# Gathering diagonal blocks by DMA in a DeltaNet encoder block, with DVE's order and the inversion's place changed

## The chip, the cores and the metric

The kernel runs on one core of one Trainium2 chip. The core's engines are TensorE (PE, with its weight loads PEld), VectorE (DVE), ScalarE (ACT), GpSimd (POOL) and SyncE (SP); transfers are issued here from SP's queue and, for some, from ACT's. The metric is the device time of one execution in microseconds. The kernel before took a median of 1217.43 us in three runs (1215.95 to 1219.03).

## The reference

The input is one sequence of 1024 tokens with 1024 channels in float32. One layer is computed:

```
xn   = rmsnorm(x)
proj = xn @ w_in                     # 1024 x 2832: attention q, k, v; gated DeltaNet q, k, v, z; gates a, b
attn = windowed attention, 8 heads of 64, 2 key/value heads, window 128, bias and sink
gdn  = two gated DeltaNets (forward and backward), 4 heads of 128, chunks; rmsnorm, times silu(z)
h    = x + concat(attn, gdn) @ w_out
out  = rmsnorm(h + relu(rmsnorm(h) @ w_ffn_in)^2 @ w_ffn_out)
```

The part that the change touches is the preparation of the DeltaNet, for each chunk, head and direction:

```
decay = exp(gc[i] - gc[j])           # on and below the diagonal
A     = beta * (k k^T) * decay       # strictly below the diagonal
T     = inverse(I + A)
P     = (q k^T) * decay
```

T and P are then used by a scan over the chunks.

## The kernel before

The kernel works with chunks of 128 tokens, eight of them, four heads and two directions. Products are made in three float32r passes: each operand is split into a rounded part and a remainder, and `mm3` (lines 136 to 138) multiplies high by high, high by low and low by high. Banks of PSUM come in two groups of four, psA and psB.

After the norms, the gates and the projections of DeltaNet's k and q, `phases` runs two streams of Python generators woven together (`weave`). Each yields a cost after each piece; the stream whose sum of costs, divided by its weight, is smaller is traced next.

- The first stream (weight 145) traces 28 projections, each of 24 matmuls into a psA bank, each yielding 5.2: eight for DeltaNet's v (`proj_conv`; copied from PSUM by ACT at line 404, convolved by DVE at 383 and 385, Silu on ACT at 387, transposed at 424, scaled at 464), eight for z (`proj_z`; Silu from PSUM at 473), four for attention's keys and values and eight for its queries (`proj_attn`; PSUM is left by DVE at 491 for keys and values, at 509 for queries). `proj_attn` first zeroes the unused halves of two key tiles, on DVE (486).
- The second stream (weight 100) traces `prep`, `eliminate`, `diag_blocks` and `invert` for its steps 0 and 1 (chunks 0 to 3); steps 2 and 3 come later, beside attention. Its yields sum to 24 for `prep`, 25.9 for `eliminate` and 4.8 for `diag_blocks`.

`prep` goes over the chunks. For each it computes k k^T (649) and q k^T (651) in two psB banks, and for each direction the decay's exponents in another (656, 657); ACT takes the exponential (661), DVE makes A (665, tile `at`), stores it to a DRAM tensor `atd` (672), and multiplies the decay with q k^T (673, which also reads the second bank for the last time in direction 1), stored to `pd` (674). The four 32 x 32 blocks on A's diagonal are copied by ACT (670, four copies for each chunk and direction, each 32 partitions x 4 heads x 32) to a tile `diag` for each direction.

`eliminate` transposes `diag` in 32 x 32 blocks on DVE (682), so that all 32 blocks of a partition group lie along the free axis, and inverts them together in 31 steps of a product and a subtraction on DVE (691, 693). `diag_blocks` transposes the result back, in two forms (702, 703). `invert` combines the blocks to the full inverses with small products: it loads A from `atd` (724), multiplies 32 x 32 blocks (750), copies them out by ACT (753), writes the diagonal blocks in place by ACT and DVE (734), multiplies again (766, 770), and goes on to 64 x 64 blocks (792, 800).

The instructions are not issued as traced. At the end of tracing, a planner that simulates the time of each instruction puts every engine's instructions in an order: of those that are ready in the simulation, the one traced first. On the chip each engine, and each queue of transfers, follows its order without exception, and waits where the order has an instruction whose inputs are late. `tc.issue_after(i)` ties instructions behind `i` on the same engine in that order; `behind` does this for a list.

Of the kernel before, what the change touches and what calls it, by code (L numbers as in the profile page):

```python
# [14 lines left out]
ALU = mybir.AluOpType  # L15
AX = mybir.AxisListType

P = 128
# [55 lines left out]
def chain(*gens):  # L74
    for g in gens:
        yield from g


class Block:
# [187 lines left out]
    def gemm(self, ws, xs, pstag):  # L267
        ps = self.ps(pstag)
        for k in range(NK):
            self.mm3(ps, ws[0][:, k, :], ws[1][:, k, :], xs[k][:, 0], xs[k][:, 1], k == 0, k == NK - 1)  # L270
        return ps
# [205 lines left out]
    def proj_attn(self):  # L477
# [6 lines left out]
        self.kh, self.kl = [self.pg(dt=F32R) for _ in range(2)], [self.pg(dt=F32R) for _ in range(2)]  # L484
        for v, o in enumerate((up, lo)):
            nc.vector.tensor_copy(out=self.kl[v][o, :], in_=self.zero[o, :].to_broadcast([64, SEQ]))
        self.va = self.pg((P, NT, P))
# [154 lines left out]
    def prep(self):  # L642
        nc = self.nc
        self.diag = [self.pg((P, 32, 32)) for _ in range(2)]
        for c in range(NT):
            sl = slice(c * P, (c + 1) * P)
            gg, kq = self.ps("psB", (P, GH, P)), self.ps("psB", (P, GH, P))
# [4 lines left out]
            for d in range(2):  # L652
# [10 lines left out]
                for h in range(GH):  # L663
# [3 lines left out]
                                                   op0=ALU.mult, op1=ALU.mult)  # L667
                for q in range(4):
                    r = slice(32 * q, 32 * q + 32)
                    nc.scalar.copy(out=self.diag[d][r, :, 4 * c:4 * c + 4].rearrange("p i h -> p h i"),  # L670
                                   in_=at[r, :, r])
                nc.sync.dma_start(out=self.atd[c, :, d], in_=at)
                nc.vector.tensor_tensor(out=dec, in0=dec, in1=kq, op=ALU.mult)
                nc.sync.dma_start(out=self.pd[c, :, d], in_=dec)
                yield 1.5

    def eliminate(self):

        nc = self.nc
        m, t = self.dbl((P, 2, 32, 32)), self.dbl((P, 2, 32, 32))  # L680
        for d in range(2):
            nc.vector.transpose(out=m[:, d].rearrange("p a b -> p b a") if d else m[:, d], in_=self.diag[d])
        nc.gpsimd.memset(t.rearrange("p d a b -> p (d a b)"), 0.0)
# [23 lines left out]
    def invert(self, tt, steps):  # L707
# [10 lines left out]
        for i in steps:  # L718
# [3 lines left out]
            for d in range(2):  # L722
                a = both[:, d]
                nc.sync.dma_start(out=a, in_=self.atd[2 * i:2 * i + 2, :, d].rearrange("c p h x -> p c h x"))
                at.append(flat(a))
                mk = {(0, 1): self.wh, (0, 2): self.wl}.get((d, i))
                tt[d][i] = mk((P, 2, GH, P), F32) if mk else self.pg((P, 2, GH, P))
                nc.gpsimd.memset(tt[d][i].rearrange("p c h x -> p (c h x)"), 0.0)
# [17 lines left out]
            for n in range(8):  # L746
                for j in range(2):
                    for d in range(2):
                        s, e = pairs[d][j]
                        nc.tensor.matmul(px[blk(e), n, :], at[d][blk(s), n, blk(e)], ct[d][blk(s), :, 8 * i + n],  # L750
                                         start=True, stop=True)
            x32 = self.pt((P, 8, 32))
# [553 lines left out]
    def build(self):  # L1306
        tc, nc = self.tc, self.nc
        with (
# [14 lines left out]
            self.kvd = d("kvd", (NT, P, 2, GH, P))[:]  # L1323
            self.pd, self.atd = d("pd", (NT, P, 2, GH, P))[:], d("atd", (NT, P, 2, GH, P))[:]
            self.phases()

    def phases(self):
# [11 lines left out]
        for half in range(2):  # L1339
# [5 lines left out]
            else:  # L1345
# [16 lines left out]
        run(weave((chain(self.proj_conv(C_GV, "v"), self.proj_z(), self.proj_attn()), 145.0),  # L1362
                  (chain(self.prep(), self.eliminate(), self.diag_blocks(), self.invert(tt, (0, 1))), 100.0)))
        self.bias_table()
# [91 lines left out]
```

## Time and profile before

| what | us |
|---|---|
| median of 3 runs | 1217.43 (1215.95 to 1219.03) |
| profiled execution, whole | 1216.62 |
| its span, first to last instruction | 1214.9 |
| PE busy | 1171.8 |
| DVE busy | 855.4 |
| ACT busy | 610.2 |
| POOL busy | 560.5 |
| mean granted clock of TensorE | 0.989 of full |

In the profile a time of an instruction is counted from the first instruction of the execution. An engine's idle time before an instruction is put down to what ended it: "[1.73 <-DVE pt L673]" says that the engine was idle for 1.73 us until an instruction of DVE at line 673, which writes a tile `pt`, was done. Names are the program's own, without buffer numbers: psA and psB are the two groups of PSUM banks, pg, pt, sc, wr, wh, wl and dbl groups of buffers. An engine's name with a q stands for its sequencer, where transfers are issued. The granted clock is a share of TensorE's full clock.

### The profile page before, as it was taken

What the parts mean: (1) busy time and instruction counts of PE and PEld (TensorE: products, weight loads), DVE (VectorE), ACT (ScalarE), POOL (GpSimd) and SP (SyncE); (2) the same over time, 40 slices, a digit from 0 to 9 for tenths busy, and PEclk for the clock granted to TensorE, in tenths of its full rate; (3) what the DMA queues carried; (4) which work ended last, traced back from release to release, by engine and by line L of the source; (5) the groups of instructions that cost most, each with busy time, mean ns of one, the idle gap of its engine ahead of it and who ended that gap; (6) DMA issues with size and microseconds to landing.
All of it is one profiled execution on the core that took longest, in us unless ns stands there. A gap on an engine that the chain in (4) does not pass through costs nothing. (4 is left out here: it accounts for less than half of the span.)

```text
span 1214.9 us, 18460 instructions
## 1 busy us (share of the span) xinstructions
PE 1171.8 (96%) x6482; PEld 960.9 (79%) x6482; DVE 855.4 (70%) x1482; ACT 610.2 (50%) x1331; POOL 560.5 (46%) x470
## 2 busy tenths in 40 slices
PE   6999999899979989999999999999999999999997
PEld 5788878677868778888788888888878888888885
DVE  4676667994399986687855445454598796987976
ACT  6455588424385752134745454454555444334443
POOL 5354311223421224143854453635456565555695
PEclk9999999899989999999999999999999999999999
DMA  6134344433645567323143444344779535443323
GB/s 246 53 102 145 89 167 163 157 123 97 219 138 176 187 203 274 121 96 122 53 166 130 157 154 156 134 153 147 244 277 333 184 104 173 135 156 109 104 87 139
DMA packets 121630, 187.62 MB, mean 154 GB/s; under 512 B 11043, under 2 KB 64416, under 8 KB 121537
## 3 DMA queue, kind: packets, MB, share of 16 engines
q1 hardware_dynamic: 103876, 155.20, 38.7%
q10 hardware_dynamic: 17661, 31.24, 6.8%
q8 instruction: 51, 0.84, 0.3%
q14 instruction: 42, 0.34, 0.1%
HBM read 122.39 MB, written 63.49 MB: 153 GB/s over the span
## 5 line engine op out<-in xcount | busy, mean ns | idle before, releaser
L136 PE MATMUL psA<-pg,wh 128*128 128x512 f32 x416 | 165.6, 399 | 3.4 <-DVE pt L491 1.7
L138 PE MATMUL psA<-pg,wl 128*128 128x512 f32 x416 | 164.8, 396 | 0.0
L137 PE MATMUL psA<-pg,wh 128*128 128x512 f32 x416 | 164.5, 395 | 0.0
L124 POOL TENSOR_TENSOR wl<-wr,wh 128x512 fp32r<-128x512 f32 x44 | 67.0, 1544 | 156.1 <-ACT wh L123 126.9
L1225 DVE TENSOR_TENSOR pg<-pg 128x512 fp32r<-128x512 f32 x112 | 122.3, 1125 | 14.9 <-ACT pg L1224 14.9
L124 POOL TENSOR_TENSOR wh<-wr,wh 128x512 fp32r<-128x512 f32 x32 | 47.4, 1498 | 139.6 <-ACT wh L123 131.3
L1142 ACT ACTIVATE pt<-pt 128x512 f32<-128x512 f32 x64 | 40.4, 632 | 121.2 <-DVE pt L1132 121.1
L136 PE MATMUL psA<-pg,pg 128*128 128x512 f32 x256 | 98.7, 391 | 0.8 <-DVE pg L1270 0.8
L137 PE MATMUL psA<-pg,pg 128*128 128x512 f32 x256 | 99.3, 391 | 0.0
L138 PE MATMUL psA<-pg,pg 128*128 128x512 f32 x256 | 99.2, 389 | 0.0
L136 PEld LDWEIGHTS psA<-pg,wh 128*128 128x128 f32 x416 | 78.9, 190 | 20.9 <-ACT pt L473 2.1
L137 PEld LDWEIGHTS psA<-pg,wh 128*128 128x128 f32 x416 | 79.0, 190 | 18.0 <-issue 0.9
L138 PEld LDWEIGHTS psA<-pg,wl 128*128 128x128 f32 x416 | 78.9, 190 | 17.0
L124 POOL TENSOR_TENSOR pg<-wr,pg 128x512 fp32r<-128x512 f32 x48 | 73.8, 1571 | 38.1 <-ACT pg L123 38.1
L1224 ACT CAST pg<-pg 128x512 fp32r<-128x512 f32 x112 | 66.9, 620 | 38.0 <-DMA pg<-sd 31.3
L137 PE MATMUL psB<-pg,pg 128*128 128x512 f32 x192 | 74.9, 390 | 0.8 <-POOL pg L124 0.7
L138 PE MATMUL psB<-pg,pg 128*128 128x512 f32 x192 | 74.7, 389 | 0.0
L136 PE MATMUL psB<-pg,pg 128*128 128x512 f32 x192 | 74.7, 389 | 0.0
L1132 DVE TENSOR_TENSOR pt<-psB,pt 128x512 f32<-128x512 f32 x39 | 26.9, 689 | 58.9 <-PE psB L138 40.6
L123 ACT CAST wh<-wr 128x512 fp32r<-128x512 f32 x76 | 43.6, 623 | 48.3 <-PE psA L137 27.7
L1132 DVE TENSOR_TENSOR pt<-psA,pt 128x512 f32<-128x512 f32 x39 | 26.8, 688 | 52.2 <-PE psA L138 35.2
L136 PEld LDWEIGHTS psA<-pg,pg 128*128 128x128 f32 x256 | 48.0, 188 | 12.1 <-DVE pg L1270 2.1
(395 smaller groups left out, 3234.1 us busy)
## 6 DMA issues: line engine op xcount, KB each, us to landing
sd<-pt ACTq DMA_DIRECT2D x112, 256.0 KB, 2.0
pg<-sd SPq DMA_DIRECT2D x112, 256.0 KB, 2.9
wr<-in_w_ffn_in SPq DMA_DIRECT2D x32, 512.0 KB, 3.6
wr<-in_w_in SPq DMA_DIRECT2D x22, 512.0 KB, 3.9
pg<-in_x SPq DMA_DIRECT2D x16, 512.0 KB, 4.5
wr<-in_w_ffn_out SPq DMA_DIRECT2D x16, 512.0 KB, 5.1
sc<-kvd SPq DMA_DIRECT2D x14, 512.0 KB, 4.7
kvd<-pt SPq DMA_DIRECT2D x16, 256.0 KB, 2.4
```

Source lines behind the costliest of these rows:

```text
L123: a = nc.scalar.copy(out=h, in_=raw)
L124: b = (eng or nc.gpsimd).tensor_tensor(out=l, in0=raw, in1=h.bitcast(F32), op=ALU.subtract)
L136: nc.tensor.matmul(ps, wh, xh, start=first, stop=False, skip_group_check=onto)
L137: nc.tensor.matmul(ps, wh, xl, start=False, stop=False, skip_group_check=onto)
L138: return nc.tensor.matmul(ps, wl, xh, start=False, stop=last, skip_group_check=onto)
L1132: self.nc.vector.tensor_tensor(out=out, in0=in0, in1=in1, op=ALU.add)
L1142: self.nc.scalar.activation(out=c, in_=c, func=AF.Relu)
L1224: nc.scalar.copy(out=s[:, 0], in_=raw)
L1225: v.tensor_tensor(out=s[:, 1], in0=raw, in1=s[:, 0].bitcast(F32), op=ALU.subtract)
```

## The change

The tile `diag` is laid out with the block index ahead of the column, and `atd` with direction and partition ahead of the chunk. The stores to `atd` are unchanged in size; the loads in `invert` now read two chunks of a partition in one run.

The copies by ACT stay only for chunk 6. For chunks 0 to 3 the diagonal blocks are read back from `atd` by eight transfers on SP's queue, traced at the start of chunk 5; for chunks 4 and 5 by eight more, traced at the start of chunk 7. For chunk 7 each direction has four transfers from the tile `at` itself. Each moves runs of 32 elements (128 bytes).

The two transposes in `eliminate`, and the zeroing of the key tiles, are tied behind the last multiplication of `prep` (line 673 of the kernel before, now `self.decayed`) in DVE's order.

The inversion's steps are traced later by 16 units of the second stream, and the first products of its step 0 are tied, in PE's order, behind the last matmul of the projection traced last.

```diff
@@ gemm
-            self.mm3(ps, ws[0][:, k, :], ws[1][:, k, :], xs[k][:, 0], xs[k][:, 1], k == 0, k == NK - 1)
+            m = self.mm3(ps, ws[0][:, k, :], ws[1][:, k, :], xs[k][:, 0], xs[k][:, 1], k == 0, k == NK - 1)
+        self.projected = m.ins
         return ps
@@ proj_attn
-        for v, o in enumerate((up, lo)):
-            nc.vector.tensor_copy(out=self.kl[v][o, :], in_=self.zero[o, :].to_broadcast([64, SEQ]))
+        with self.tc.issue_after(self.decayed):
+            for v, o in enumerate((up, lo)):
+                nc.vector.tensor_copy(out=self.kl[v][o, :], in_=self.zero[o, :].to_broadcast([64, SEQ]))
@@ prep
         for c in range(NT):
+            if c in (5, NT - 1):
+                a, b = (0, 4) if c == 5 else (4, 6)
+                for d in range(2):
+                    for q in range(4):
+                        r = slice(32 * q, 32 * q + 32)
+                        nc.sync.dma_start(out=self.diag[d][r, 4 * a:4 * b, :],
+                                          in_=self.atd[d, r, a:b, :, r].rearrange("p c h x -> p (c h) x"))
...
-                for q in range(4):
+                nc.sync.dma_start(out=self.atd[d, :, c], in_=at)
+                for q in range(4 if c > 5 else 0):
                     r = slice(32 * q, 32 * q + 32)
-                    nc.scalar.copy(out=self.diag[d][r, :, 4 * c:4 * c + 4].rearrange("p i h -> p h i"),
-                                   in_=at[r, :, r])
-                nc.sync.dma_start(out=self.atd[c, :, d], in_=at)
-                nc.vector.tensor_tensor(out=dec, in0=dec, in1=kq, op=ALU.mult)
+                    if c == 6:
+                        nc.scalar.copy(out=self.diag[d][r, 4 * c:4 * c + 4, :], in_=at[r, :, r])
+                    else:
+                        nc.sync.dma_start(out=self.diag[d][r, 4 * c:4 * c + 4, :], in_=at[r, :, r])
+                self.decayed = nc.vector.tensor_tensor(out=dec, in0=dec, in1=kq, op=ALU.mult).ins
@@ eliminate
-        for d in range(2):
-            nc.vector.transpose(out=m[:, d].rearrange("p a b -> p b a") if d else m[:, d], in_=self.diag[d])
+        with self.tc.issue_after(self.decayed):
+            for d in range(2):
+                nc.vector.transpose(out=m[:, d].rearrange("p a b -> p b a") if d else m[:, d],
+                                    in_=self.diag[d].rearrange("p x i -> p i x"))
@@ invert
-                nc.sync.dma_start(out=a, in_=self.atd[2 * i:2 * i + 2, :, d].rearrange("c p h x -> p c h x"))
+                nc.sync.dma_start(out=a, in_=self.atd[d, :, 2 * i:2 * i + 2])
...
-                        nc.tensor.matmul(px[blk(e), n, :], at[d][blk(s), n, blk(e)], ct[d][blk(s), :, 8 * i + n],
-                                         start=True, stop=True)
+                        with self.behind([self.projected] if i == 0 else []):
+                            nc.tensor.matmul(px[blk(e), n, :], at[d][blk(s), n, blk(e)], ct[d][blk(s), :, 8 * i + n],
+                                             start=True, stop=True)
@@ build
-            self.pd, self.atd = d("pd", (NT, P, 2, GH, P))[:], d("atd", (NT, P, 2, GH, P))[:]
+            self.pd, self.atd = d("pd", (NT, P, 2, GH, P))[:], d("atd", (2, P, NT, GH, P))[:]
@@ phases
-                  (chain(self.prep(), self.eliminate(), self.diag_blocks(), self.invert(tt, (0, 1))), 100.0)))
+                  (chain(self.prep(), self.eliminate(), self.diag_blocks(), iter((16.0,)),
+                         self.invert(tt, (0, 1))), 100.0)))
```

## The prediction

> **What bounds the kernel now.** I read the page first, then the busy time by stretch around the stages that the change touches, then in each stall the instructions in order of time, then the groups of ACT and DVE.
>
> ```profile
> span 1214.9 us, 18460 instructions
> PE 1171.8 (96%) x6482; PEld 960.9 (79%) x6482; DVE 855.4 (70%) x1482; ACT 610.2 (50%) x1331; POOL 560.5 (46%) x470
> ```
>
> PE, at 96%, is the bound. So the change is worth what it takes from PE's idle time and from PE's time at a low granted clock, and nothing else. The stretches show where these lie (columns: length, busy time with number of instructions of PE, its weight loads, DVE, ACT and POOL, then the granted clock, the DMA share and GB/s):
>
> ```profile
> 139.00:214.60 75.60, 74.98 (x403) 61.04 (x401) 55.36 (x102) 63.94 (x151) 18.69 (x16) 1.00 0.46 147
> 214.60:222.00 7.40, 3.13 (x17) 1.97 (x16) 5.92 (x11) 7.28 (x18) 4.64 (x5) 0.78 0.87 276
> 222.00:225.60 3.60, 3.56 (x9) 2.82 (x10) 3.42 (x9) 1.45 (x3) 0.00 (x0) 0.51 0.50 163
> 225.60:267.50 41.90, 41.90 (x191) 34.42 (x193) 39.88 (x62) 4.71 (x9) 7.00 (x5) 1.00 0.34 112
> 267.50:272.00 4.50, 2.33 (x162) 2.06 (x161) 4.41 (x6) 4.35 (x8) 3.33 (x4) 1.00 0.66 233
> 272.00:276.80 4.80, 4.80 (x14) 3.81 (x15) 2.95 (x7) 4.47 (x8) 1.87 (x2) 0.64 0.25 58
> ...
> 327.30:337.80 10.50, 7.74 (x217) 6.58 (x216) 9.94 (x40) 8.57 (x24) 4.00 (x6) 1.00 0.60 179
> 337.80:348.50 10.70, 9.00 (x120) 7.96 (x120) 8.57 (x29) 7.79 (x25) 2.95 (x3) 0.52 0.02 6
> ```
>
> While prep runs (139 to 214.6) PE is full, so relief of ACT there gives PE nothing directly. There are two stalls. *Stall 1*, at the end of prep: PE idles 7.40 - 3.13 = 4.3 us. *Stall 2*, at the end of the elimination: 4.50 - 2.33 = 2.2 us. Behind each the clock is low, and what that costs is seen on a matmul row at 222.63 and one at 226.06:
>
> ```profile
> 214.85 0.66 PE L424 MATMUL psB<-ident,sc 128*128 128x128 f32 x4 [0.20 <-ACT pt L661]
> 215.88 0.66 PE L424 MATMUL psB<-ident,sc 128*128 128x128 f32 x4 [0.38 <-ACT pt L661]
> 216.86 0.66 PE L424 MATMUL psB<-ident,sc 128*128 128x128 f32 x4 [0.32 <-DVE pt L665]
> 219.25 1.11 PE L424 MATMUL psB<-ident,sc 128*128 128x128 f32 x4 [1.73 <-DVE pt L673]
> 222.04 0.80 PE L136 MATMUL psA<-pg,wh 128*128 128x512 f32 x1 [1.68 <-ACT pt L473]
> 222.63 0.63 PE L137 MATMUL psA<-pg,wh 128*128 128x512 f32 x1
> ...
> 226.06 0.40 PE L137 MATMUL psA<-pg,wh 128*128 128x512 f32 x1
> ```
>
> A 512-column matmul took 0.63 us against 0.40, and the four transposes 1.11 against 0.66. Since matmuls overlap, the pace is read from the stretches: nine in 3.60 us against 191 in 41.90, 0.40 against 0.22 us each, so half clock takes 0.45 of its time away: 0.45 + 0.45 x 3.6 = 2.1 us behind stall 1, and 0.45 x 3.5 = 1.6 us behind stall 2 (3.5 us at half clock give the mean of 0.64 over 4.8). The two stalls are worth 4.3 + 2.1 + 2.2 + 1.6 = **10.2 us**; that is all the change can reach.
>
> Stall 1 has two parts that come from order. The last transposes wait 1.73 us for L673, and the next projection 1.68 us for L473. DVE and ACT at that point:
>
> ```profile
> 217.37 1.25 DVE L682 STREAM_TRANSPOSE dbl<-pg 128x1024 f32<-128x1024 f32 x1 [0.56 <-ACT pg L670]
> 218.54 0.65 DVE L673 TENSOR_TENSOR pt<-pt,psB 128x512 f32<-128x512 f32 x1
> 220.11 1.92 DVE L682 STREAM_TRANSPOSE dbl<-pg 128x1024 f32<-128x1024 f32 x1 [0.92 <-ACT pg L670]
> 222.12 0.26 DVE L691 TENSOR_TENSOR pt<-dbl,dbl 128x62 f32<-128x62 f32 x1
> ```
> ```profile
> 202.43 3.37 ACT L670 COPY pg<-pt 32x128 f32<-32x128 f32 x8
> ...
> 215.67 1.67 ACT L670 COPY pg<-pt 32x128 f32<-32x128 f32 x4
> 217.37 1.14 ACT L123 CAST wh<-wr 128x512 fp32r<-128x512 f32 x2
> 218.41 1.67 ACT L670 COPY pg<-pt 32x128 f32<-32x128 f32 x4
> 220.09 1.28 ACT L473 ACT_TABLE_LOAD   x1
> ```
>
> The last multiplication, L673, which frees the bank, stands behind a transpose, L682, that itself waited for ACT's copies; L473, which frees a projection's bank, stands behind eight such copies and a table load.
>
> Stall 2:
>
> ```profile
> PE psA L136 <- DVE pt L491: 1.7, 1, 1.7
> PE psB L766 <- ACT pt L753: 0.5, 1, 0.5
> ```
> ```profile
> 267.52 3.68 DVE L734 COPY pg<-sc 32x256 f32<-32x256 f32 x4
> 271.23 0.69 DVE L491 COPY pt<-psA 128x512 f32<-128x512 f32 x1
> ```
> ```profile
> L136 PE MATMUL psA<-pg,wh 128*128 128x512 f32 x64 | 25.8, 403 | 1.7 <-ACT pt L473 1.7
> ```
>
> PE runs 3 x 64 matmuls, eight projections, from 222.0 to 267.5; the last four are the key and value ones, whose results stay in all four psA banks until DVE reaches L491, and DVE is in the elimination until 267.5 and then in L734. So PE and DVE now run dry together: PE at 267.5 for want of a bank, DVE's elimination at the same moment.
>
> **The change, part by part.**
>
> *Copies taken from ACT.* Of 64 L670 copies 56 go (all but chunk 6's), 56 x 0.418 = 23.4 us:
>
> ```profile
> L670 ACT COPY pg<-pt 32x128 f32<-32x128 f32 x64 | 26.7, 418 | 4.1 <-DVE pt L665 3.6
> ```
> ```profile
> L665 DVE SCALAR_TENSOR_TENSOR pt<-pt,cc,psB 128x128 f32<-128x128 f32 x64 | 17.9, 339 | 13.6 <-ACT pt L661 13.5
> ```
>
> How much earlier prep then ends is not in the trace. Lower end: 3.4 us, the eight copies at 202.43, which stand straight before chunk 6's exponentials, with no idle time before them. Upper end: 13.5 us, all that DVE ever waited for L661. I take 5, near the low end, because DVE too was full before chunk 5 with the convolutions.
>
> *Stall 1.* Without the copies ACT's table load can follow L123 at about 217, and L473 ends near 219 instead of 222; with the transposes tied behind it, L673 runs at about 217 and not 218.5. Of the idle 4.3 us there stay the three waits inside chunk 7 (0.20 + 0.38 + 0.32) and some 0.5 us: 2.9 us come back, and the clock's 2.1 if the shorter idle keeps it up. Together 5.0 us; PE then finishes the eight projections at 262.5.
>
> *Gathers.* 24 DMAs go on SP's queue: eight for chunks 0 to 3 (64 KB each), eight for 4 and 5 (32 KB), eight from SBUF for chunk 7 (16 KB). All move pieces of 128 bytes; no row has that. The nearest:
>
> ```profile
> pt<-pt SPq DMA_DIRECT2D x4, 128.0 KB, 2.4
> ...
> wr<-in_w_in SPq DMA_DIRECT2D x1, 64.0 KB, 4.8
> ...
> grow<-gcd SPq DMA_DIRECT2D x1, 48.0 KB, 1.8
> L672 SPq DMA_DIRECT2D atd<-pt x16: 319/320/496, 149.8 to 216.8; - x16
> DMA to landing us min/median/max: 2.0/2.0/5.7
> ```
>
> An issue takes 0.32 to 0.50 us, so eight hold SP 2.6 to 4 us; what waits behind them there (the next weights, the pd stores) has no reader on PE within that time as long as stall 1's projection, whose weights ACT split at 217.4, keeps its place. Landing lies between 1.8 us (48 KB in 256-byte rows) and 4.8 us (64 KB in 64-byte rows, at the start under load). For chunks 0 to 3 and 4 to 5, issued one or two chunks ahead, I count no cost: prep's next chunks cover it. Without that cover it is the lateness of rival B.
>
> *The last chunk.* It is on the path to the elimination: before, from the end of L665 (216.8) to L691 (222.1), 5.3 us. Now the store and four issues (5 x 0.32 to 0.50), a landing of 2.0 to 2.4, and the transposes, which read a strided block:
>
> ```profile
> L703 DVE STREAM_TRANSPOSE sc<-dbl 128x1024 f32<-128x1024 f32 x2 | 4.1, 2057 | 0.0
> L486 DVE CAST pg<-zero 64x1024 fp32r<-64x1024 f32 x2 | 2.3, 1171 | 0.4 <-PE psB L651 0.3
> ```
>
> L703 reads strided and takes 2.06 us; L682 writing strided took 1.92 and dense 1.25. The second transpose strides on both sides: 2.06 to 2.7 us (2.06 plus the 0.67 that striding the writes cost). L486's 2.3 us, tied behind the last L673, fill the wait for the landing together with the first transpose. Sum 6.0 to 8.5, so 0.7 to 3.2 us more than before; I take 1.5.
>
> *Elimination and inversion.* The elimination's own time does not change. It ends at 267.5 - 5 + 1.5 = 264.0. The inversion is traced 16 units later in the weave, that is behind the twentieth projection, the last key and value one: its stream has then yielded (24 + 25.9 + 4.8 + 16) / 100 = 0.707, which the other reaches with 20 x 5.2 / 145 = 0.717 (before: 0.547, 16 projections), so the L491 copies now come before L734. The ninth projection starts at 264.0 + 0.7 = 264.7 instead of 271.97: 7.3 us, of which the second half of the small products still has to run (the 2.33 us that PE works from 267.5 to 272.0 are L750's, 1.1, and those of L766 and L770, 1.2): 6.1. PE idles 264.7 - 262.5 - 1.1 = 1.1 us there, short enough to keep the clock: + 1.6. Less 0.5 for a remaining wait on ACT's L753: **7.2 us**.
>
> *Layout of atd.* Inversion loads read 4 KB runs and not 2 KB; they were landed before use, so nothing.
>
> A rule bears on the clock. The rows show half clock for 3.5 us after idle stretches of 0.49 and 1.68 us. The Trainium skill, "TensorE: Matmul & The Clock Gate", section "What's actually happening", gives an idle window of about 3.4 us before the clock falls. By it neither stall should have cost clock, and the return would be 7.2 - 2.1 - 1.6 = 3.5 us, an estimate of 1213.9 in all; this trace does not agree, so I keep the terms.
>
> **The sum.** The profiled execution took 1216.62 us (span 1214.9 and 1.7 around it), 0.8 under the median of 1217.43. 1216.62 - 7.2 = 1209.4, and in terms of the median **1210.2 us**. Its own range: with all 10.2 back 1207, with prep only 3.4 us earlier and the chain 3.2 longer some 3.5 back, 1213.7.
>
> **Rivals.**
>
> *B, the gathered blocks land late (slower).* If the gathers run one after another at the 64-byte row's 4.8 us, the sixteen from DRAM need 77 us where the last three chunks give 3 x (216.8 - 139) / 8 = 29, and the elimination waits. It decides once the elimination starts over 3 us later than 222.1. With the longest atd landing (5.7 instead of 2.4) and 2.1 us behind a weight load on SP, it ends near 272.8, the ninth projection starts at 273.5 (+1.5), L766 follows (+1.2), and PE idles some 9 us, with 6.8 us of half clock behind it (3.2 against 1.6): +4.3, **1221.7**. Against it: the 48 KB row's 1.8 us, and that lateness up to 4 us falls into DVE's free time. The Trainium skill, "DMA: Bandwidth & Descriptors", sections "Specifications" and "Rules for kernel authors", speaks for it: below 512 bytes a transfer loses line rate, and under 64 KB it is mostly overhead. No run here shows 128-byte pieces.
>
> *C, prep does not end earlier.* ACT's relief goes into other waits (DVE's convolutions, the planner's new order), while the longer last chunk stays. Then the elimination ends at 269.0; the ninth projection starts 2.3 us earlier, less 1.2, less 0.8 of clock (some 6 us idle before it, so a longer half clock than now): **1217.1**. For it: PE and DVE were nearly full before 214.6. Against it: ACT is busy 63.94 of 75.60 us in prep and 7.28 of 7.40 at its end.
>
> *D, the gain is given back where attention begins.* The stretches from 327.3 to 348.5 idle 2.8 + 1.7 us and run at 0.52. If the new order doubles that idle time, 4.5 of the 7.2 go: **1214.7**. Against it: the work there hangs on PE's last projections and moves with them.
>
> **How the numbers follow.** What one measurement tells from no change is 0.3%, 3.7 us: 1213.8 and 1221.1. Forecast 0.60, C 0.16, D 0.11, B 0.13. The forecast lies below 1213.8, and D in a fifth of it: faster 0.62. C and the rest of D: same 0.25. B: slower 0.13. The range leaves B out and reaches past C: 1205 (2 us for small waits nobody has named) to 1219.
>
> **What would show it.** Right: no wait of PE for L673 or L473 over 0.5 us at prep's end, L691 starting before 219, L491 ahead of L734, the stretch after the fourth key and value projection under 1.5 us idle and at full clock. Wrong: a first L691 later than 222; transposes idle before themselves on a DMA for over 3 us; a new half-clock stretch between 200 and 350 longer than the old ones.

## The result and the profile after

The changed kernel takes 1226.17 us (median of nine runs, 1222.74 to 1230.09), the kernel before 1218.33 beside it; the ratio is 1.0074 (95% interval 1.006 to 1.0088). The forecast was 1210.2. The change costs some 9 us where 7 were to be gained. The profiled execution took 1225.43 us. All times and ratios here and below are of runs in the fast state; a single run of late_only that took 2120.17 us is left out.

The first lines of the page after:

```profile
span 1223.7 us, 18440 instructions
PE 1171.0 (96%) x6482; PEld 959.3 (78%) x6482; DVE 868.7 (71%) x1482; ACT 586.7 (48%) x1275; POOL 562.0 (46%) x470
```

PE's work is what it was (1171.8 before), and the span is 8.8 us longer: PE stands idle. Busy time by stretch after (columns as in the prediction):

```profile
213.90:217.20 3.30, 2.30 (x18) 1.75 (x16) 3.22 (x7) 3.07 (x5) 2.40 (x2) 1.00 0.50 157
...
255.40:264.10 8.70, 0.06 (x1) 0.06 (x1) 8.43 (x13) 3.51 (x6) 5.68 (x5) 0.61 0.13 30
264.10:267.60 3.50, 3.50 (x11) 2.92 (x12) 3.33 (x6) 0.00 (x0) 1.89 (x3) 0.51 0.02 5
...
279.10:283.50 4.40, 0.03 (x1) 0.03 (x1) 4.23 (x6) 0.14 (x1) 2.87 (x4) 0.74 0.68 234
283.50:288.10 4.60, 4.60 (x74) 3.71 (x75) 1.29 (x2) 3.40 (x7) 0.00 (x0) 0.51 0.02 4
```

Stall 1 is nearly gone: 3.30 - 2.30 = 1.0 us idle against 4.3, and the clock stays up. PE's next projection starts at 217.20 and not at 222.04. (Below it is projection 29, counted in the order of tracing from DeltaNet's k; keys and values are 33 to 36, the queries 37 to 44.) Then come two stops that the kernel before does not have, 8.7 us from 255.4 and 4.4 us from 279.1, each with half clock behind it. DVE is full in both. PE in order of time:

```profile
264.04 1.11 PE L425 MATMUL psB<-ident,pt 128*128 128x128 f32 x4 [8.68 <-DVE pt L493]
...
283.47 0.90 PE L425 MATMUL psB<-ident,pt 128*128 128x128 f32 x3 [4.39 <-DVE pt L493]
```

L425 are the transposes of attention's values (L424 before), and L493 (L491 before) is DVE's copy of a key or value projection out of PSUM. DVE in order of time:

```profile
232.51 0.56 DVE L704 TENSOR_TENSOR pt<-dbl,dbl 128x384 f32<-128x384 f32 x1
...
234.95 1.59 DVE L704 TENSOR_TENSOR pt<-dbl,dbl 128x440 f32<-128x440 f32 x1
...
256.87 0.68 DVE L493 COPY pt<-psA 128x512 f32<-128x512 f32 x1
...
258.71 1.50 DVE L704 TENSOR_TENSOR pt<-dbl,dbl 128x384 f32<-128x384 f32 x1
...
261.78 0.52 DVE L704 TENSOR_TENSOR pt<-dbl,dbl 128x350 f32<-128x350 f32 x1
...
263.30 0.68 DVE L493 COPY pt<-psA 128x512 f32<-128x512 f32 x1
...
270.17 1.25 DVE L715 STREAM_TRANSPOSE sc<-dbl 128x1024 f32<-128x1024 f32 x1
...
276.98 0.69 DVE L493 COPY pt<-psA 128x512 f32<-128x512 f32 x1
277.57 5.12 DVE L747 COPY pg<-sc 32x256 f32<-32x256 f32 x8
282.72 0.69 DVE L493 COPY pt<-psA 128x512 f32<-128x512 f32 x1
```

The copies for the two value projections are the second and the fourth L493. The second (263.30) stands inside the elimination (L704, L706), where PE, 6.5 us ahead of its old times, gets to it early and waits; the fourth (282.72) stands behind the elimination's four transposes (from 270.17) and behind the eight diagonal copies L747. The step at 258.71 takes 1.50 us, one of the same 384 elements at 232.51 took 0.56. The elimination's products as a group, before and after (x: min/median/max ns, first and last start):

```profile
L691 DVE TENSOR_TENSOR pt<-dbl,dbl x31: 224/558/1670, 222.1 to 260.6; 128x62 f32<-128x62 f32 x2, 128x120 f32<-128x120 f32 x2, 128x174 f32<-128x174 f32 x2, 128x224 f32<-128x224 f32 x2
```
```profile
L704 DVE TENSOR_TENSOR pt<-dbl,dbl x31: 225/592/1649, 224.3 to 269.6; 128x62 f32<-128x62 f32 x2, 128x120 f32<-128x120 f32 x2, 128x174 f32<-128x174 f32 x2, 128x224 f32<-128x224 f32 x2
```

It starts 2.2 us later and takes 45.3 us, and not 38.5, from its first product to its last. POOL in that time, first after, then before, and last the two slow steps of the kernel before:

```profile
234.39 3.30 POOL L124 TENSOR_TENSOR wl<-wr,wh 128x512 fp32r<-128x512 f32 x2 [14.16 <-ACT wh L123]
239.83 3.19 POOL L124 TENSOR_TENSOR wl<-wr,wh 128x512 fp32r<-128x512 f32 x2 [2.14 <-DMA wr<-in_w_in]
258.28 3.05 POOL L501 TENSOR_TENSOR pg<-pt,pg 64x512 fp32r<-64x512 f32 x2 [15.26 <-ACT pg L499]
261.39 2.73 POOL L741 MEMSET pg<- 128x1024 f32 x3
265.73 2.67 POOL L124 TENSOR_TENSOR wl<-wr,wh 128x512 fp32r<-128x512 f32 x2 [1.61 <-PE psA L138]
```
```profile
241.17 3.48 POOL L124 TENSOR_TENSOR wl<-wr,wh 128x512 fp32r<-128x512 f32 x2 [20.45 <-ACT wh L123]
```
```profile
241.83 1.67 DVE L693 TENSOR_TENSOR dbl<-dbl,pt 128x512 f32<-128x512 f32 x1
243.53 1.67 DVE L691 TENSOR_TENSOR pt<-dbl,dbl 128x510 f32<-128x510 f32 x1
```

Eight two-input POOL operations (remainders of weights, L124, and of keys, L501) run beside the elimination's steps after, two before. PE's lead brings some of them there: its buffers come free sooner, so the next weights are split sooner. The later inversion brings them too, by the order; the experiments below part the two. Each slows one DVE step by about 1 us; the MEMSETs from 261.39 on slow none (0.52 at 261.78).

Last, the end of prep after: DVE, then SP's queue:

```profile
215.52 4.55 DVE L488 CAST pg<-zero 64x1024 fp32r<-64x1024 f32 x2
219.99 4.18 DVE L694 STREAM_TRANSPOSE dbl<-pg 128x1024 f32<-128x1024 f32 x2
224.28 0.27 DVE L704 TENSOR_TENSOR pt<-dbl,dbl 128x62 f32<-128x62 f32 x1
```
```profile
213.55 2.65 SPq L683 DMA_DIRECT2D pg<-pt  x4
...
216.94 0.38 SPq L677 DMA_DIRECT2D atd<-pt  x1
217.36 2.54 SPq L683 DMA_DIRECT2D pg<-pt  x4
```

From the last A (L674, ended 214.8) to the first step of the elimination it is 9.5 us, against 5.3 before: the eight transfers issue one behind the other, with stores between the two directions, and the zeroing takes 4.55 us. DVE has no idle time in these 9.5 us, so here it waits for no transfer.

### The profile page after: what moved, and what is told of

The parts are those of the page before. It is cut to its first block, busy times and chain, and to the rows that moved or that the text cites. A ratio compares the mean times of both kernels' runs of the same rounds, so it can differ in the third digit from the quotient of the medians.

```text
span 1223.7 us, 18440 instructions
## 1 busy us (share of the span) xinstructions
PE 1171.0 (96%) x6482; PEld 959.3 (78%) x6482; DVE 868.7 (71%) x1482; ACT 586.7 (48%) x1275; POOL 562.0 (46%) x470
## 4 chain that ended last, share of the span: by engine, by line
PE 59%; DVE 6%; issue 2%; DMA 2%; ACT 1%; POOL 1%; SPq 0%; POOLq 0%; ACTq 0%; DVEq 0%
PE psA L136 9%; PE psA L137 9%; PE psA L138 9%; PE psB L136 8%; PE psB L137 8%; PE psB L138 8%; PE psB L852 5%; PE psA L602 2%; PE psA L590 1%; DMA pg<-sd 1%; POOL pg L124 1%; DVE pt L1248 1%; PE psA L558 1%; DVE wr L1251 1%; DVE pg L1284 1%
## 5 line engine op out<-in xcount | busy, mean ns | idle before, releaser
L1239 DVE TENSOR_TENSOR pg<-pg 128x512 fp32r<-128x512 f32 x112 | 124.8, 1149 | 12.5 <-ACT pg L1238 12.5
L124 POOL TENSOR_TENSOR wl<-wr,wh 128x512 fp32r<-128x512 f32 x44 | 66.3, 1529 | 140.6 <-ACT wh L123 120.1
L124 POOL TENSOR_TENSOR wh<-wr,wh 128x512 fp32r<-128x512 f32 x32 | 47.3, 1498 | 139.8 <-ACT wh L123 139.8
L124 POOL TENSOR_TENSOR pg<-wr,pg 128x512 fp32r<-128x512 f32 x48 | 73.3, 1558 | 37.9 <-ACT pg L123 37.9
L1146 DVE TENSOR_TENSOR pt<-psA,pt 128x512 f32<-128x512 f32 x39 | 26.8, 689 | 52.7 <-PE psA L138 35.3
```

Source lines behind the costliest of these rows:

```text
L124: b = (eng or nc.gpsimd).tensor_tensor(out=l, in0=raw, in1=h.bitcast(F32), op=ALU.subtract)
L1146: self.nc.vector.tensor_tensor(out=out, in0=in0, in1=in1, op=ALU.add)
L1239: v.tensor_tensor(out=s[:, 1], in0=raw, in1=s[:, 0].bitcast(F32), op=ALU.subtract)
```

## The experiments

Two theories were set against each other. **E**: what sets the loss is the time at which DVE is through with the elimination; PE waits for it wherever it needs DVE next, so PE's lead is worth nothing. **O**: the loss is an accident of order, value transposes and copies at bad places. The ratio is that of each kernel's time to that of the kernel before, run beside it. The code cuts are shortened.

| kernel | median us | ratio | 95% interval |
|---|---|---|---|
| no_late | 1221.89 | 1.0036 | 1.0019 to 1.0054 |
| late_only | 1219.59 | 1.0025 | 1.0007 to 1.0042 |
| pool_one_input | 1224.73 | 1.0063 | 1.0044 to 1.0081 |
| v_later | 1222.75 | 1.0046 | 1.0028 to 1.0064 |
| c7_act | 1219.21 | 1.0017 | 1.0003 to 1.0031 |
| ties_only | 1220.74 | 1.0046 | 1.0028 to 1.0064 |
| gather_only | 1222.59 | 1.0053 | 1.0033 to 1.0073 |
| kvL24 | 1223.07 | 1.0056 | 1.0036 to 1.0076 |
| pga_kvL24 | 1219.33 | 1.0016 | 1.0004 to 1.0029 |
| pga_kvL28 | 1206.91 | 0.9917 | 0.9896 to 0.9939 |
| short7 | 1222.60 | 1.0046 | 1.0028 to 1.0064 |
| bk28 | 1216.99 | 0.9997 | 0.9982 to 1.0013 |
| pool_all | 1218.03 | 1.0008 | 0.9995 to 1.0020 |
| t28 | 1213.90 | 0.9985 | 0.9971 to 0.9998 |
| g28 | 1207.38 | 0.9932 | 0.9909 to 0.9955 |
| kvL28_c7 | 1209.57 | 0.9939 | 0.9924 to 0.9955 |

### The parts of the change, and other orders

*no_late*: the change without the later inversion.

```diff
-    iter((16.0,)), self.invert(tt, (0, 1))
+    self.invert(tt, (0, 1))
-    with self.behind([self.projected] if i == 0 else []):
```

> The changed kernel with the gathers and the ties, but the inversion traced where it was before (no 16 units ahead of it, no tie of its first products to a projection). Theory O (order): what costs is the order that the later inversion brings, value transposes of the projections 33 and 34 at projection 35 in PE's order, where PE waits 8.7 and 4.4 us for DVE's copies. Taken away, PE has the old order again and only the longer elimination against it: at most 1218. Theory E (elimination): what costs is that the elimination ends 9 us later whatever the order, and PE waits for it wherever it has to; here projections 33 to 36 fill the four banks, their copies stand behind the elimination and the diagonal copies in DVE's order, PE idles some 13 us: 1221 to 1224. Both: elimination 224 to 272 or later, first L704 at 224.

*late_only*: the later inversion alone, on the kernel before.

```diff
-    self.invert(tt, (0, 1))
+    iter((16.0,)), self.invert(tt, (0, 1))
+    with self.behind([self.projected] if i == 0 else []):
```

> The kernel before with the later inversion alone (16 units and the tie of the first products), ACT's 64 diagonal copies as before, no gathers, no ties. Theory O: the value transposes come to projection 35 as in the changed kernel and PE waits there for DVE's copies that stand inside the elimination: 1223 to 1228. Theory E: the elimination starts at 222 and takes 46 to 48 us, PE is not ahead of DVE at that point and the banks are released in time: 1212 to 1216.

*v_later*: the value transposes of `proj_attn` written two projections later.

```diff
-                pv = self.transposed(t, 0)
-                nc.vector.tensor_copy(out=self.va[:, 4 * half:4 * half + 4, :], in_=pv)
+                values.append((half, t))
...
+                if values and (i, half) in ((1, 0), (1, 1)):
+                    vh, vt = values.pop(0)
+                    pv = self.transposed(vt, 0)
+                    nc.vector.tensor_copy(out=self.va[:, 4 * vh:4 * vh + 4, :], in_=pv)
```

> The changed kernel, with the value transposes (and the copy of their result) written two projections later in the key and value loop; then in PE's order they stand behind projection 38 and not at 35 and 37, and the inversion's first products stand ahead of them, behind projection 36. Theory O: the 8.7 and 4.4 us before the transposes go, little comes in their place: about 1217. Theory E: PE, ahead of DVE, now waits at the products behind projection 36 for the end of the elimination: 1224 to 1228.

The first line of PE's waits in this stage, in no_late and in v_later:

```profile
PE psB L762 <- DMA dbl<-atd: 11.1, 2, 10.1
```
```profile
PE psB L768 <- DMA dbl<-atd: 11.5, 1, 11.5
```

The value transposes no longer hold PE, and PE waits 11 us elsewhere, at the inversion's first products, for the load of A. That load goes into a `dbl` buffer which the elimination's factors hold until its last step. This speaks for E; O was right in that the order of the changed kernel is worse by some 3 to 5 us (1.0074 against 1.0046 and 1.0036). late_only came between both forecasts: with PE not ahead, the third copy comes inside the elimination, and PE's waits after 225 are as short as before; its 3 us are not accounted for by the one profile.

late_only also shows that POOL does not come beside the elimination through PE's lead alone. PE's projection 29 starts there as late as before, and yet eight of the steps are slow, beside operations of which the kernel before has most only after its steps, from 262.6 on:

```profile
246.86 3.31 POOL L124 TENSOR_TENSOR wl<-wr,wh 128x512 fp32r<-128x512 f32 x2 [2.22 <-DMA wr<-in_w_in]
254.78 3.17 POOL L500 TENSOR_TENSOR pg<-pt,pg 64x512 fp32r<-64x512 f32 x2 [4.61 <-ACT pg L498]
```

In no_late, with PE's lead and without the later inversion, six are slow. Either part of the change does it.

*gather_only* and *ties_only* are the kernel before with the gathers, layout and chunk 6's copies alone, and with the two ties alone.

> The kernel before with the gathered diagonal blocks (transfers for six chunks and the last, ACT for chunk 6, new layout) alone: no ties, inversion where it was. Theory E: the last chunk's transfers hold the elimination's start at about 224, PE's earlier projections bring POOL's remainders into the elimination, which ends at 267 or later and holds PE for 8 to 10 us: 1219 to 1222, as with the ties. If the ties are to blame for the loss that was measured with both: 1213 to 1217.

> The kernel before with the two ties alone (zeroing and the elimination's transposes behind the last multiplication), no gathers, inversion where it was. The 1.73 us wait for the last multiplication goes, the 1.68 us wait for ACT's activation behind the copies stays; the elimination starts 1 to 2 us later (223 to 224) because zeroing comes ahead of the transposes. Theory E: PE gains under 2 us there and gives it back at the end of the elimination: 1215 to 1218. If the ties do what the forecast said: 1213 or less.

gather_only loses no less than no_late, by the same wait (10.6 us for that load). In ties_only the last multiplication comes 1.9 us earlier, as meant, and the zeroing, tied behind it, takes 2.99 us between the two transposes (before it ran at 211.3, where DVE waited anyway); the elimination starts at 223.5 and not at 222.1, while ACT's activation stays where it was:

```profile
218.54 2.99 DVE L487 CAST pg<-zero 64x1024 fp32r<-64x1024 f32 x2
```

That explains why nothing is gained; the loss of 0.46% is more than E allowed, and where the rest of it lies stays open.

### The elimination's start and length

*c7_act*: the last chunk's blocks copied by ACT.

```diff
-                    if c == 6:
+                    if c > 5:
```

> The changed kernel with the last chunk's diagonal blocks copied by ACT as chunk 6's are, in place of the eight transfers on SP; the order is else the same, value transposes at projections 35 and 37. Theory E (the elimination's end sets when PE goes on): the last chunk's chain, 9.5 us with the transfers, is 5.5 to 6.5, the elimination starts at 221 instead of 224.3 and ends 3 us earlier, PE's waits at the value transposes are 3 us shorter in sum: 1221 to 1223. If the waits came from the order alone: 1224 to 1226.

It gained more than E said, 7 us. The elimination starts at 221.6, and the third copy, which the changed kernel has behind the transposes, comes inside it; the fourth stands ahead of the diagonal copies:

```profile
275.51 0.66 DVE L493 COPY pt<-psA 128x512 f32<-128x512 f32 x1
276.08 3.07 DVE L747 COPY pg<-sc 32x256 f32<-32x256 f32 x8
```

PE's waits for the copies fall from 13.1 to 3.7 us, and 1.9 us more idle time at prep's end is paid for it. The elimination's end is not what did it: nine of its steps are slow, and its closing transposes begin at 269.45, only 0.7 us earlier than in the changed kernel, where E expected 3. The place of the copies did. The eight transfers of the last chunk thus hurt twice: by the time that they take, and by the order that follows from it.

*pool_one_input* and *pool_all*: in the changed kernel's own order, POOL's remainders beside the elimination come from one input. The cut shows the weights; it applies to the splits 15 to 18 in pool_one_input and 15 to 22 in pool_all, where the keys' remainders (L501) are replaced too.

```diff
-            self.split(view(raws[kh]), hh, ll)
+            self.nc.scalar.copy(out=hh, in_=view(raws[kh]))
+            self.nc.gpsimd.tensor_scalar(out=ll, in0=hh.bitcast(F32), scalar1=0.0, scalar2=None, op0=ALU.mult)
```

> The changed kernel in its own order, but the remainders (second halves) of the splits of the last z weights and of the key and value weights, which POOL computes from two inputs during the elimination, are replaced by a POOL operation of one input that gives zero; these remainders are left out of the computation. If POOL's two-input operations slow DVE's elimination steps beside them (1.5 to 1.65 us in place of 0.6), the elimination falls from 52 us to 46 to 48. Theory E then: 1217 to 1220. Theory O: the copies stay where they stand, PE still waits for the copies, though less: 1221 to 1223. If POOL is not the cause, the elimination stays at 52 us and the time at 1225 to 1227.

> The changed kernel in its own order, with all of POOL's two-input operations that fall into the elimination (remainders of the last z, key, value and first query weights, and of the keys) replaced by POOL operations of one input that give zero; these remainders are left out of the computation. Theory P: the eight steps of 1.3 to 1.65 us fall back to 0.3 to 0.67, the elimination's steps are 8 us shorter (46 to 38), the value copy of the second projection comes 4 us earlier and the fourth copy 8 us earlier: PE's 13.1 us of waiting fall to 3 to 7, time 1214 to 1219. Rival: not POOL, but DVE's order alone: steps remain slow or the time stays at 1223 to 1226.

pool_one_input replaced only one of the four pairs beside the elimination, and came out 1.3 us lower, which the intervals don't tell from nothing. pool_all replaced all. Both also replaced the pair beside the zeroing, which then took 1.70 us and not 4.55. POOL there, and the same DVE steps:

```profile
234.13 3.46 POOL L268 TENSOR_SCALAR wl<-wh 128x512 fp32r<-128x512 f32 x2 [13.80 <-ACT wh L267]
```
```profile
234.00 0.62 DVE L710 TENSOR_TENSOR pt<-dbl,dbl 128x440 f32<-128x440 f32 x1
234.66 0.91 DVE L712 TENSOR_TENSOR dbl<-dbl,pt 128x440 f32<-128x440 f32 x1
```

POOL works as long as before (3.46 us for two), and the DVE steps beside it take 0.62 and 0.91 us, where the changed kernel has 1.59 and 1.59. From its first step to its transposes the elimination lasts 40.6 us in place of 45.9 (with the copies inside it), and it starts 0.9 us earlier; PE's two waits are 4.0 and 0.9 us, and the time falls by 0.66%, 8.0 us: nearly the whole loss. That c7_act took back 6.9 with more slow steps is no contradiction: what PE waits for is the time at which DVE reaches the copies, and both faster steps and a better place in the order bring it forward.

*short7*: seven steps of the elimination cut to one element.

```diff
             rr, xx = slice(k + 1, 32), slice(0, k + 1)
+            if 11 <= k < 18:
+                rr, xx = slice(k + 1, k + 2), slice(0, 1)
```

> The changed kernel with seven of the elimination's 31 steps (the twelfth to the eighteenth) cut to one element each; the rest of these seven steps is left out of the computation. In the changed kernel these steps took 0.62 to 0.69 us each, 14 of them some 9 us; cut, 0.1 each, so the elimination ends 8 us earlier. Theory E (the elimination's end alone sets the loss): PE's waits of 8.7 and 4.4 us at the value transposes fall to about 5 in sum: 1213 to 1217, the time before or less. Rival: the order itself, the gathers or attention's start carry the loss: 1221 to 1225.

A miss for E as it was put: the elimination ended at 260.3, some 10 us earlier, and only 3.4 us came back. The planner had moved the second copy from inside the elimination to behind its transposes, together with the third:

```profile
266.26 1.25 DVE L493 COPY pt<-psA 128x512 f32<-128x512 f32 x2
```

PE waits for it 9.8 us in one stop. So the end of the elimination alone doesn't set the loss: it is the time at which DVE reaches the copies, and that is a matter of its speed and of its order.

### Taking DVE out of PE's way

If PE's lead is lost to copies that stand in DVE's order, it should be kept when ACT, idle in the elimination, makes them, and when the inversion's products come after the elimination. *kvL24*:

```diff
-            nc.vector.tensor_copy(out=t, in_=ps)
+            nc.scalar.copy(out=t, in_=ps)
...
-                nc.vector.tensor_copy(out=self.va[:, 4 * half:4 * half + 4, :], in_=pv)
+                nc.scalar.copy(out=self.va[:, 4 * half:4 * half + 4, :], in_=pv)
...
-    iter((16.0,))
+    iter((24.0,))
```

> The changed kernel with the key, value and transposed value copies out of PSUM moved from DVE to ACT, which is nearly idle in the elimination, and the inversion 24 units later instead of 16, so that its first products stand behind projection 38. Theory E: PE then needs nothing of DVE from projection 33 to 38; it reaches the products at 273 to 275, the elimination without the two copies in it ends with its transposes at 273 to 275, so PE idles 0 to 4 us where it idled 13, and stays at full clock most of the time: 1209 to 1214, faster than both. If the loss lies elsewhere (gathers, attention's start): 1218 to 1224.

It did not: PE waited 12.4 us. ACT, and SP's queue:

```profile
276.72 1.26 ACT L500 CAST pg<-pt 64x512 fp32r<-64x512 f32 x2 [18.00 <-DMA pt<-pt]
```
```profile
270.59 0.82 SPq L737 DMA_DIRECT2D dbl<-atd  x2
271.50 0.47 SPq L496 DMA_DIRECT2D pt<-pt  x1
```

The same load of A waits at the head of SP's queue for its buffer until 270.6; the transfers that swap the keys' halves stand behind it; ACT waits for them, and PE for ACT. *pga_kvL24* and *pga_kvL28* give the load buffers of its own:

```diff
-            both = self.dbl((P, 2, 2, GH, P))
+            both = self.dbl((P, 2, 2, GH, P)) if i else None
             for d in range(2):
-                a = both[:, d]
+                a = both[:, d] if i else self.pg((P, 2, GH, P))
```

> As kvL24 (key, value copies on ACT, inversion 24 units later), and the inversion's first two loads go into buffers of their own instead of the one that the elimination's factors hold until its last step. In kvL24 that load stood at the head of SP's queue for 24.3 us, the swap transfers of the keys behind it, ACT's L500 waited 18.0 us for them, ACT's value copy and PE behind that, 12.4 us. Theory Q (the elimination holds PE through SP's queue): the 12.4 us go, PE idles 0 to 4 us at the products behind projection 38: 1209 to 1214. Rival: something else of DVE's or ACT's order holds PE until the elimination's end all the same: 1217 to 1223.

> As pga_kvL24 with the inversion 28 units later, its first products behind projection 40. Theory Q: PE does not idle between 217 and the end of projection 40; the inversion ends later against the projections, so some of its latency falls behind the last projection, 2 to 4 us: 1209 to 1214. If the inversion's latency then decides attention's start: 1214 to 1220.

The wait of 12.4 us is gone in both, but not quite as thought: SP's queue is still held to 272.4, now by the load for the inversion's second step, and ACT's L500 waits longer than ever. What has changed is ACT's order: the last value copy stands ahead of that cast, as in pga_kvL28:

```profile
262.00 0.58 ACT L493 COPY pt<-psA 128x512 f32<-128x512 f32 x1
281.87 1.27 ACT L500 CAST pg<-pt 64x512 fp32r<-64x512 f32 x2 [19.30 <-DMA pt<-pt]
```

In pga_kvL24 PE runs on to 272.4 and then waits, at the products behind projection 38, for the elimination, which now has twelve POOL operations beside it and ends at 272.6 (its transposes at 278.4; the profile names DVE's L511, which comes right behind them), and for the load:

```profile
279.79 0.28 PE L764 MATMUL psB<-sc,pg 32*32 32x32 f32 x2 [7.43 <-DVE pt L511]
281.76 1.11 PE L764 MATMUL psB<-sc,pg 32*32 32x32 f32 x62 [1.69 <-DMA pg<-atd]
```

Two projections later there is nothing left to wait for. Stretches of pga_kvL28:

```profile
217.00:255.40 38.40, 38.40 (x172) 31.80 (x172) 36.99 (x47) 9.54 (x18) 13.35 (x10) 1.00 0.43 139
255.40:283.30 27.90, 27.90 (x129) 22.78 (x131) 24.57 (x30) 6.17 (x12) 9.25 (x6) 1.00 0.35 114
283.30:313.30 30.00, 30.00 (x483) 24.32 (x483) 14.59 (x29) 17.90 (x31) 16.56 (x18) 1.00 0.56 187
```

PE is busy without a gap and at full clock from 217.0 to the end of the last projection at 313.3 (327.3 before), though the elimination is longer than in the changed kernel (48.3 us against 45.3 from the first product to the last). This kernel beats both: 0.9917, and at 1206.91 us lies below its forecast of 1209 to 1214. Whether it needs the load's own buffers wasn't tried.

What the change is worth there was asked of four kernels with these three edits: on the kernel before (*bk28*), with the ties alone (*t28*), the gathers alone (*g28*), both (pga_kvL28), and both but for the last chunk's transfers (*kvL28_c7*, edited as c7_act).

> The kernel before, without gathers and ties, with the three edits of pga_kvL28: key and value copies on ACT, inversion 28 units later behind projection 40, first inversion loads in buffers of their own. It tells what gathers and ties are worth once the elimination holds PE no more. By the forecast's term for stall 1 (2.9 us idle and 2.1 of clock) it is 5 us slower than pga_kvL28: 1210 to 1213. If gathers and ties bring nothing even then: 1205 to 1208.

> bk28 with the two ties alone. The 1.7 us wait of the last transposes goes, the 1.7 us wait for ACT's activation behind copies and table load grows to 3 to 4 as in ties_only; the elimination's start, 1.5 us later, has slack. So nothing gained: 1215 to 1218. If the ties are what brought the 10 us: 1206 to 1210.

> bk28 with the gathers alone (and ACT's copies for chunk 6 alone). ACT's activation comes 3 us earlier, PE's projection 29 starts at 217 instead of 222 and at full clock, as in gather_only: nearly all of the 10 us: 1206 to 1209. If the ties share in it: 1210 to 1214.

> pga_kvL28 with the last chunk's blocks copied by ACT instead of transfers. The elimination starts 3 us earlier, which is worth nothing now, but ACT's activation stands behind eight copies again and PE waits 2.9 us with half clock behind it as in c7_act: 4 to 6 us slower than pga_kvL28, 1211 to 1213. If the earlier elimination still counts: 1204 to 1207.

Against bk28 (0.9997) the ties bring 0.12%, which the intervals don't tell from nothing, the gathers 0.65% or 7.9 us, both 0.80% or 9.7 us. The three edits alone bring nothing (bk28), so with them the change is worth about twice the 5 us that bk28's forecast gave it. The last chunk's transfers, which cost 7 us in the changed kernel, are 2.7 us ahead here, which the overlapping intervals don't settle: their late elimination has slack now, and ACT's earlier activation counts. It is less than forecast because the half clock that was expected behind PE's 2.9 us in kvL28_c7 did not come:

```profile
219.30:223.00 3.70, 3.67 (x16) 3.04 (x17) 3.60 (x5) 1.45 (x3) 0.00 (x0) 1.00 0.00 0
```

In c7_act it did come behind a stop of the same length (0.50 from 219.30 to 223.00).

## Why the prediction was wrong

**Stall 1: right, and its cause.** Of the 2.9 us of idle time and 2.1 us of clock that were to come back, 3.3 and all of the clock did. PE's projection started 4.84 us earlier, by the step named: L474 (L473 before) out from behind ACT's copies. Its size was right too: between the profiles of bk28 and pga_kvL28 the idle time there falls from 4.1 to 1.0 us, and 2.1 us of clock go, 5.2 in all. The rest of the 8.9 us between these two profiles lies elsewhere, above all in the clock from 300 to 365 (mean 0.92 and 0.97, some 3 us), which the prediction did not have.

**Prep 5 us earlier: too much.** The last A ended at 214.8 instead of 216.8. The 2.0 us lie below the lower bound of 3.4, which took for granted that the eight copies before chunk 6's exponentials were in the way; ACT in fact stood idle before the last chunk's exponentials:

```profile
211.61 2.18 ACT L670 ACTIVATE pt<-psB,ngc 128x128 f32<-128x128 f32 x8 [2.33 <-issue]
```

These exponentials start right behind PE's product of their exponents, and that came only 0.9 us earlier than before (after, then before):

```profile
211.14 0.38 PE L666 MATMUL psB<-maskb,identb 128*128 128x512 bf16 x1
```
```profile
212.00 0.38 PE L657 MATMUL psB<-maskb,identb 128*128 128x512 bf16 x1
```

PE was full in prep, 74.98 of 75.60 us before and 74.90 of 74.90 after. The prediction had seen that, and took ACT's relief as time all the same.

**The last chunk, +1.5 us (0.7 to 3.2): +4.2.** Two terms were mis-sized. The zeroing took 4.55 us where 2.3 were counted, because of what POOL does beside it (last section); that is the one that bound here. An issue of these transfers took 0.60 us, where the nearest rows had 0.32 to 0.50, with 1.2 us of stores between the two directions; this lies close behind, for in pool_all, where the zeroing took 1.70 us, the second transpose waited 1.60 us for a transfer and the first step came only 0.9 us earlier. The sum was off as well: the terms that it lists, issues of 1.6 to 2.5, a landing of 2.0 to 2.4 and a second transpose of 2.06 to 2.7, make 5.7 to 7.6 and not 6.0 to 8.5.

**"The elimination's own time does not change": the step that failed.** It ends, with its transposes, at 276.4 where 264.0 was forecast. 5.7 us of that are its start (224.3 for 218.6), 6.7 its length: 1.2 us for two copies now inside it, and nearly all the rest POOL, with eight slow steps against two at about 1 us each. pool_all, where each one-input operation still cost 0.3 to 0.4, took 5.3 us off this length. The kernel before had the evidence, two steps of 1.67 us at 241.8 and 243.5 beside POOL's L124; the prediction asked of PE's lead, and of the later inversion, only what they give PE, not which engine they set to work beside DVE.

The Trainium skill, "SBUF — State Buffer", section "Who interferes with whom", says that a DVE instruction with two inputs in SBUF contends with a GpSimd instruction that reads SBUF, and not with one that only writes. The rows agree: 0.9 to 1.1 us more beside a POOL operation of two inputs, 0.3 to 0.4 us beside one of one input, none beside a MEMSET.

**"The L491 copies now come before L734": half, and the second step that failed.** Two came inside the elimination, one behind its transposes, one behind the diagonal copies. PE was held not at the ninth projection for a bank but within the third key and value projection, at a transpose of the one before it, which the prediction did not have. In place of 1.1 us of idle time there are 13.1. In pga_kvL28, which takes these copies off DVE and puts the products later, PE does not wait there at all.

**The clock.** Behind the two new stops PE ran some 8 us at half clock, 3.5 and 4.6. Stall 1's 1.0 us left the clock up. At half clock a microsecond costs half of it, so these 8 us cost 4.0, against the 2.1 + 1.6 behind the two stalls before. The clock thus adds next to nothing to the loss: PE's busy time, in which slow matmuls count in full, is 0.8 us less than before, while PE's idle time over the whole span is 52.7 us against 43.1. (The mean granted clock, 0.987 against 0.989 in the profiles, counts idle stretches too, as the 0.61 over the 8.70 us from 255.4.) The Trainium skill's window of about 3.4 us of idle time ("TensorE: Matmul & The Clock Gate", "What's actually happening") holds for these stops of 4.4 and 8.7 us, and for the 1.0 us that cost no clock; the kernel before lost it behind two stops of 1.73 and 1.68 us in a row, which that page's rule does not give.

**The gathers' landing and the layout: right.** The transfers from DRAM (L653) landed in 2.2 us in the median, 6.7 at most, and held up nothing.

**The rivals.** B had the right sign with half the size (1221.7, 4.3 us slower, against some 9) and a wrong reason: no transpose of the changed kernel waited for a transfer. Its 272.8 also counts from the old end, 267.5, without the 5 us that prep was to gain. C's point, prep not earlier, was nearer than the forecast. The rival that was missing is the one that came: PE's lead turns into waiting, because the engine that it must wait for gets slower and not faster.

## What to carry to other kernels

Before an engine is put ahead, ask where it meets the next engine, and whether that one can keep the pace: relief at one stage is worth what the next meeting point lets through, here nothing until the copies, the load and the products were taken out of DVE's way. An engine in front also pulls other engines' work forward, and so does a new place in the order; look what that work then runs beside. An in-order queue with one transfer that waits for a buffer holds all behind it, so a buffer that a long stage keeps should not be the target of an early load.

## What the runs showed of the hardware

Beside a two-input operation of POOL, a DVE product or subtraction of two SBUF tiles took 0.9 to 1.1 us longer (0.62 to 1.59 at 440 elements), once for each POOL operation; with one input on POOL's side it was 0.3 to 0.4. A cast on DVE could suffer more: half of the zeroing took 0.68 to 0.69 us with nothing beside it (gather_only), 1.11 to 1.81 beside L124 (the first half in the changed kernel, the second in the kernel before, both in ties_only), and 3.42 where a MEMSET of POOL followed L124 (the changed kernel, 216.6 to 220.1); beside a POOL operation of one input the halves took 0.69 and 0.99 (pool_all). The Trainium skill, "SBUF — State Buffer", section "Who interferes with whom", counts casts among the operations that can hold DVE and GpSimd off each other whole; these rows fit that. No run varied the MEMSET alone.

A transfer issued on SP from SBUF to SBUF in 128-byte pieces held the queue for 0.60 us in the median (L683), against 0.34 for the store L677 of 256 KB; the gathers from DRAM held it 0.47 (L653).

A stop of PE of 2.9 us was followed by half clock in c7_act and by full clock in kvL28_c7. Stops of 1.0 us were not followed by half clock.
